# Low parts of the later weights by an accumulating DMA onto the negated high part, in place of a VectorE subtraction

## The chip, the cores and the metric

The kernel runs on one core of one Trainium2 chip. The metric is the device time of one execution in microseconds. A profile of one execution stands beside it: busy times of the engines (PE is TensorE's matmuls, DVE is VectorE, ACT is ScalarE, POOL is GpSimd, SP is SyncE, which only issues DMAs), waits, and the chain of work that ended last.

## The reference

One decoder block over 1024 tokens of width 1024, with a stick-breaking attention branch and a pooling branch. Cut to what matters here:

```python
h = rms_norm(x, norm_gain) * (1.0 + scale) + shift
proj = h @ w_in                                  # (1024, 1024) @ (1024, 8192)
q, k, v, z_a, u, z_b, m_a, m_b = split(proj)
attn = stick_breaking_attention(heads(q), heads(k), heads(v))
p_a = (attn * silu(z_a)) @ w_branch_a
p_b = (multiscale_causal_pool(u) * silu(z_b)) @ w_branch_b
out = x + gate * ((sigmoid(m_a) * p_a + sigmoid(m_b) * p_b) @ w_out)
return rms_norm(out, final_gain)
```

## The kernel before

**Products in two parts.** Every matrix is kept as a high part, the value rounded to the float32r format, and a low part, value minus high. A product is three matmuls into one sum: high by high, high by low, low by high (`mm3`). A column block of `w_in` is 128 columns wide, so as a tile it is 128 partitions by 1024 numbers, 512 KB. Its product with all tokens is two halves (`sh`) of 512 tokens, each 24 matmuls into one PSUM bank.

**Stages, in the order of PE.** First h and the folded u weights, then the second half of the u products (`u7_1` down to `u0_1`), then v (16 blocks `v0_0` to `v7_1`, 24 matmuls each), then z_b (`wzb0_0`, `wzb0_1` to `wzb7_1`), then w_branch_b (`pb0_0` to `pb7_1`), then attention together with the remaining 40 column blocks of `w_in`, then the branches and the output. The results of u, v, z_b, pb and the attention projections go through a tag `pj` with two PSUM banks: a product can begin only when the one two before it has been evicted. For v, ACT casts the bank to the high part (L610, `vo`) and DVE subtracts (L611). For z_b, ACT takes the sigmoid of the bank (L635, `zs`), and DVE multiplies the bank with it (L636), which is the last read of the bank.

**Low parts made early.** Of the 40 column blocks for the attention stage, the low parts of the last 32 (`l8` to `l39`) are made while u, v, z_b and pb run. They are written to a DRAM tensor `wl_d` and read back much later (L171, from 491.5 us on). This is the job of `make_lo`. For each tile, SP loads the block into `raw` (L152); ACT casts it to `hi` (L155); DVE subtracts and leaves the low part in `raw` (L156); SP stores `raw` to `wl_d` (L157). Eight tiles are asked for beside u and ten beside v (list `LO_V`, twice), from a pool with three buffers `lraw` and one buffer `lhi`; four beside z_b (`LO_ZB`), with two `lraw` and one `lhi`; ten beside pb (`LO_PB`), where raw and hi share a ring of five buffers with the tag `d`. With one `lhi`, the next cast waits until everything that reads or writes the previous `hi` is over: before, that is the subtraction L156.

**Order.** Outside the parts that the code pins, a scheduler puts each engine's instructions into an order when the program is built, by its own estimate of when each could run. That order is then fixed: an instruction that waits holds up all that stand behind it on its engine, and a DMA whose data isn't ready holds up its issuing queue. POOL's other work in this region is the low part of the w_branch_b tiles (`wb`, L118) and little else.

Of the kernel before, what the change touches and what calls it, by code (L numbers as in the profile page):

```python
# [9 lines left out]
F32 = mybir.dt.float32  # L10
F32R = mybir.dt.float32r
AF = mybir.ActivationFunctionType
ALU = mybir.AluOpType
# [44 lines left out]
def block_kernel(ctx, tc, a, out):  # L58
    nc = tc.nc
    v, act, gp = nc.vector, nc.scalar, nc.gpsimd  # L60
# [22 lines left out]
    wl_d = dram.tile([5 * KB, P, D], F32, name="wl_d")  # L83
# [58 lines left out]
    def make_lo(pl, n, tag=None, bufs=3, later=False):  # L142

        rest = []
        for _ in range(n):
            i = next(early_lo)
            if tag:
                raw, hi = (pl.tile([P, D], t_, tag=tag, bufs=5, name=f"l{i}_{n_}") for n_, t_ in (("raw", F32), ("hi", F32R)))
            else:
                raw = pl.tile([P, D], F32, tag="lraw", bufs=bufs, name=f"l{i}_raw")  # L150
                hi = pl.tile([P, D], F32R, tag="lhi", bufs=1, name=f"l{i}_hi")
            nc.sync.dma_start(raw, a["w_in"][tiles[i]])  # L152

            def low(i=i, raw=raw, hi=hi):
                act.copy(hi, raw)  # L155
                v.tensor_sub(raw.bitcast(F32R), raw, hi.bitcast(F32))  # L156
                nc.sync.dma_start(wl_d[i], raw)  # L157

            if later:
                rest.append(low)  # L160
            else:
                low()
        return rest
# [51 lines left out]
    with pool("init") as init:  # L215
# [168 lines left out]
        hi, lo_ = (0,), (1,)  # L384
# [719 lines left out]
```

## Time and profile before

| | us |
|---|---|
| device time, median of 3 runs | 1210.2 (1209.76 to 1210.31) |
| span of the profiled execution | 1210.3 |
| PE busy in it | 1199.2 |
| DVE busy | 756.5 |
| ACT busy | 531.6 |
| POOL busy | 187.2 |
| ACT's 32 casts L155, mean of one | 1.05 |
| DVE's 32 subtractions L156, mean of one | 1.22 |

The span is the profiled execution's own time; it lies inside the range of the timed runs, so nothing has to be added to it. PE busy is a sum over all stages, and the other engines' shares are averages over stages that need them differently: the tables by stretch of time show each stage by itself. The early low parts lie between 68.8 us (first load) and about 330 us (last store). In every view below, times are counted from the start of the span.

### The profile page before, as it was taken

The numbers are of one execution on the slowest core, as the hardware profiler recorded it, in microseconds if no ns is written. First come the engines' busy times: TensorE is split into PE (matmuls) and PEld (weight loads), VectorE is DVE, ScalarE is ACT, GpSimd is POOL, SyncE is SP. The second block draws the span as 40 slices with busy tenths as digits, with TensorE's granted clock in tenths as the row PEclk, the third lists the DMA queues.
The fourth block names the chain that finished last, engine by engine and source line by source line (L and its number), as shares of the span: only waits on it lengthen the run. The fifth ranks groups of instructions, "written<-read, shape, count | busy, mean of one in ns | idle before, by whom it ended". The sixth has DMA issues, their size and how long they took to land.

```text
span 1210.3 us, 16177 instructions
## 1 busy us (share of the span) xinstructions
PE 1199.2 (99%) x5746; PEld 1002.5 (83%) x5746; DVE 756.5 (63%) x1050; ACT 531.6 (44%) x1008; POOL 187.2 (15%) x360
## 2 busy tenths in 40 slices
PE   8999999999999999999999999999999999999997
PEld 7888878888888888888888888888888888888886
DVE  5764483677510286767868677686777853785643
ACT  5564331334301255655555555655555643232211
POOL 1000000001221333212222222222221210000001
PEclk9999999999999999999999999999999999999999
DMA  9649995626847632442635325353343344975622
GB/s 358 255 171 325 328 356 207 209 87 225 309 148 120 191 91 76 124 122 86 170 109 156 113 80 153 110 157 118 102 134 101 99 131 167 353 272 170 216 67 83
DMA packets 81955, 207.14 MB, mean 171 GB/s; under 512 B 10449, under 2 KB 23889, under 8 KB 79698
## 3 DMA queue, kind: packets, MB, share of 16 engines
q1 hardware_dynamic: 73666, 191.23, 49.2%
q10 hardware_dynamic: 8208, 14.88, 3.3%
q8 instruction: 45, 0.74, 0.2%
q14 instruction: 36, 0.29, 0.1%
HBM read 138.96 MB, written 50.34 MB: 156 GB/s over the span
## 4 chain that ended last, share of the span: by engine, by line
PE 88%; DMA 5%; issue 3%; DVE 2%; ACT 1%; POOL 0%; POOLq 0%; ACTq 0%; DVEq 0%; SPq 0%
PE p L103 34%; PE pb L103 7%; PE wzb L103 7%; PE pa L103 7%; PE o L103 6%; PE z L103 6%; PE av L103 5%; PE wt L103 5%; PE v L103 4%; PE ua L103 3%; DMA wl_d<-l_raw 2%; DMA l_raw<-in_w_in 2%; PE u L103 2%; PE wm L103 1%; DVE l_raw L156 1%
## 5 line engine op out<-in xcount | busy, mean ns | idle before, releaser
L103 PE MATMUL p<-hT,w 128*128 128x512 f32 x1920 | 480.0, 391 | 0.5 <-ACT m_sg L201 0.5
L103 PEld LDWEIGHTS p<-hT,w 128*128 128x128 f32 x1920 | 355.2, 188 | 74.7 <-ACT m_sg L201 1.0
L826 DVE TENSOR_TENSOR_SCAN om<-om 128x512 f32<-128x512 f32 (+7 forms) x128 | 175.8, 1373 | 124.9 <-ACT om L819 69.4
L819 ACT ACTIVATE om<-z 128x512 f32<-128x512 f32 (+2 forms) x192 | 94.5, 492 | 155.9 <-PE z L103 133.5
L824 POOL TENSOR_SCALAR_AFFINE_SELECT om<-om 128x128 f32<-128x128 f32 x128 | 56.3, 440 | 346.5 <-ACT om L819 287.0
L846 DVE TENSOR_TENSOR wt<-wt,wt 128x512 fp32r<-128x512 f32 (+1 forms) x160 | 99.3, 621 | 16.1 <-ACT wt L845 15.5
L845 ACT CAST wt<-wt 128x512 fp32r<-128x512 f32 (+1 forms) x160 | 88.2, 551 | 48.1 <-PE wt L103 47.9
L103 PE MATMUL av<-wt,vv 128*128 128x512 f32 x320 | 106.4, 414 | 0.0
L103 DVE TENSOR_TENSOR be<-be,om 128x511 f32<-128x511 f32 (+7 forms) x128 | 95.1, 749 | 1.1 <-POOL be L824 0.7
L820 ACT ACTIVATE be<-z 128x512 f32<-128x512 f32 (+2 forms) x192 | 94.1, 490 | 0.0
L103 PE MATMUL pa<-ga,wa 128*128 128x512 f32 x384 | 89.6, 389 | 0.1
L103 PE MATMUL o<-wo,mhl 128*128 128x512 f32 (+1 forms) x408 | 89.6, 377 | 0.0
L103 PE MATMUL wt<-ident,be 128*128 128x128 f32 x576 | 89.4, 273 | 0.0
L103 PE MATMUL v<-wv,hT 128*128 128x512 f32 x384 | 87.8, 390 | 0.5 <-DVE vo L611 0.5
L103 PE MATMUL wzb<-hT,wzb 128*128 128x512 f32 x384 | 87.2, 389 | 0.0
L103 PE MATMUL pb<-gb,wb 128*128 128x512 f32 x384 | 87.2, 389 | 0.0
L103 PEld LDWEIGHTS v<-wv,hT 128*128 128x128 f32 x384 | 71.9, 188 | 16.2 <-DVE vo L611 1.4
L103 PEld LDWEIGHTS o<-wo,mhl 128*128 128x128 f32 x408 | 73.5, 188 | 14.1
L103 PEld LDWEIGHTS pa<-ga,wa 128*128 128x128 f32 x384 | 72.0, 188 | 15.4 <-DVE wa L118 0.5
L103 PEld LDWEIGHTS wzb<-hT,wzb 128*128 128x128 f32 x384 | 72.1, 188 | 14.9
L103 PEld LDWEIGHTS pb<-gb,wb 128*128 128x128 f32 x384 | 72.1, 188 | 14.9
L103 PEld LDWEIGHTS wt<-ident,be 128*128 128x128 f32 x576 | 70.2, 141 | 11.6
(130 smaller groups left out, 1364.5 us busy)
## 6 DMA issues: line engine op xcount, KB each, us to landing
w_raw<-in_w_in SPq DMA_DIRECT2D x40, 512.0 KB, 4.7
l_raw<-in_w_in SPq DMA_DIRECT2D x32, 512.0 KB, 5.2
wl_d<-l_raw SPq DMA_DIRECT2D x32, 512.0 KB, 5.7
w<-wl_d SPq DMA_DIRECT2D x32, 512.0 KB, 3.8
v_d<-vo SPq DMA_DIRECT2D x16, 512.0 KB, 5.2
vv<-v_d SPq DMA_DIRECT2D x8, 1024.0 KB, 5.3
wa_raw<-in_w_branch_a SPq DMA_DIRECT2D x16, 512.0 KB, 4.7
wa<-in_w_mod SPq DMA_DIRECT2D x7, 1024.0 KB, 6.4
```

The costliest lines, as they stand in the source:

```text
L103: ins = op(*args, **kw)
L156: v.tensor_sub(raw.bitcast(F32R), raw, hi.bitcast(F32))
L819: act.activation(om[:, b0:b0 + n], zp[:, :n], AF.Sigmoid, scale=-0.125)
L820: act.activation(be[:, b0:b0 + n], zp[:, :n], AF.Sigmoid, scale=0.125)
L824: gp.affine_select(out=tl[:, :P], in_=tl[:, :P], pattern=[[1, P]], compare_op=ALU.is_gt, fill=fill, base=0, channel_multiplier=-1)
L826: v.tensor_tensor_scan(om[:, :W], om[:, :W], om[:, :W], 1.0, ALU.mult, ALU.min)
L845: act.copy(wt[:, 0, :off], pt[:, :off])
L846: v.tensor_sub(wt[:, 1, :off], pt[:, :off], wt[:, 0, :off].bitcast(F32))
```

## The change

In `make_lo`, ACT writes the negative of the rounded tile to `hi` instead of the rounded tile. POOL then issues a DMA that adds `raw` onto `hi`, in SBUF, which leaves raw minus high in `hi`. SP stores `hi` to `wl_d`, where it stored `raw` before. DVE has no part in it any more. The pools, the numbers of buffers and the places where `make_lo` is called are the same.

```diff
             def low(i=i, raw=raw, hi=hi):
-                act.copy(hi, raw)
-                v.tensor_sub(raw.bitcast(F32R), raw, hi.bitcast(F32))
-                nc.sync.dma_start(wl_d[i], raw)
+                act.mul(hi, raw, -1.0)
+                gp.dma_start(hi.bitcast(F32), raw, accum_op=ALU.add)
+                nc.sync.dma_start(wl_d[i], hi.bitcast(F32))
```

So `hi` is now in use from the multiplication through the accumulating DMA until the store has been read out of it, and with one `lhi` the next tile's multiplication waits for the end of that store. `raw` is free when the accumulating DMA has ended.

PE's order is the same as before. On ACT, the 18 tiles `l8` to `l25` begin at the same place (behind the cast of `wv0_1`) but are spread further. This is ACT at the end of the v stage and the beginning of z_b, before:

```order
L610 CAST vo5_1_1643<-v5_1_1618 128x8x64
L610 CAST vo6_1_1675<-v6_1_1650 128x8x64
L610 CAST vo7_1_1710<-v7_1_1685 128x8x64
L155 CAST l26_hi_1857<-l26_raw_1856 128x1024
L155 CAST l27_hi_1997<-l27_raw_1996 128x1024
L635 ACTIVATE zs0_0_1722<-wzb0_0_1729 128x512
L638 CAST gb_1721<-zs0_0_1722 128x512
L635 ACTIVATE zs0_1_1723<-wzb0_1_1759 128x512
```

And now:

```order
L610 CAST vo6_1_1675<-v6_1_1650 128x8x64
L155 ACTIVATE l20_hi_1394<-l20_raw_1393 128x1024
L610 CAST vo7_1_1710<-v7_1_1685 128x8x64
L155 ACTIVATE l21_hi_1464<-l21_raw_1463 128x1024
L155 ACTIVATE l22_hi_1537<-l22_raw_1536 128x1024
L123 CAST wzb2_1866<-wzb2_raw_1864 128x1024
L155 ACTIVATE l23_hi_1572<-l23_raw_1571 128x1024
L155 ACTIVATE l24_hi_1648<-l24_raw_1647 128x1024
L155 ACTIVATE l25_hi_1680<-l25_raw_1679 128x1024
L635 ACTIVATE zs0_0_1722<-wzb0_0_1729 128x512
L635 ACTIVATE zs0_1_1723<-wzb0_1_1759 128x512
L155 ACTIVATE l26_hi_1857<-l26_raw_1856 128x1024
```

Before, tile 25 was cast ahead of the last seven evictions of v, and only tiles 26 and 27 stood here; now tiles 21 to 25, all on the one `lhi`, stand between the last eviction of v and the first of z_b.

A little further on, ACT in the z_b stage before (columns as above; `gjunk` is a sigmoid of a row needed for the output gate):

```order
L155 CAST l29_hi_2337<-l29_raw_2336 128x1024
L635 ACTIVATE zs1_1_1790<-wzb1_1_1826 128x512
L123 CAST wzb3_1933<-wzb3_raw_1931 128x1024
L638 CAST gb_1721<-zs1_0_1789 128x512
L635 ACTIVATE zs2_0_1862<-wzb2_0_1869 128x512
```

And now:

```order
L635 ACTIVATE zs1_1_1790<-wzb1_1_1826 128x512
L123 CAST wzb3_1933<-wzb3_raw_1931 128x1024
L638 CAST gb_1721<-zs1_1_1790 128x512
L155 ACTIVATE l28_hi_2165<-l28_raw_2164 128x1024
L635 ACTIVATE zs2_0_1862<-wzb2_0_1869 128x512
L638 CAST gb_1721<-zs2_0_1862 128x512
L635 ACTIVATE zs2_1_1863<-wzb2_1_1899 128x512
L123 CAST wzb4_2020<-wzb4_raw_2018 128x1024
L155 ACTIVATE l29_hi_2337<-l29_raw_2336 128x1024
L638 CAST gb_1721<-zs2_1_1863 128x512
L647 ACTIVATE gjunk_2343<-sg_2342 128x1024
L635 ACTIVATE zs3_0_1929<-wzb3_0_1936 128x512
```

Tiles 27, 28 and 29 now stand between evictions of blocks 1 and 3, one at a time; tile 29 is three half blocks later, ahead of the eviction `zs3_0`. Beyond, `l30` stands behind `zs4_1`, `l31` behind `zs5_1`, and `l39` behind the eviction of `pb2_0`.

On POOL, the difference at the only place that changes (the `st` rows belong to the first stage, the `wb` rows to pb):

```order
 L258 TENSOR_TENSOR st_638<-st_638,mhalf 128x1
+L156 DMA l_hi<-l_raw 128x1024 x25
 L118 TENSOR_TENSOR wb_2354<-wb_raw,wb_2354 128x1024
+L156 DMA l_hi<-l_raw 128x1024 x2
 L118 TENSOR_TENSOR wb_2424<-wb_raw,wb_2424 128x1024
```

25 accumulating DMAs stand ahead of the first `wb` low part, and the last seven between the `wb` low parts that follow.

## The prediction, made before the changed kernel was run

> **What bounds the kernel now.** The page comes first, then what PE waited for, then a table by stretch of time.
>
> ```profile
> span 1210.3 us, 16177 instructions
> PE 1199.2 (99%) x5746; PEld 1002.5 (83%) x5746; DVE 756.5 (63%) x1050; ACT 531.6 (44%) x1008; POOL 187.2 (15%) x360
> ```
> ```profile
> PE idle L103 <- POOL x L243: 1.6, 1, 1.6
> PE ua L103 <- ACT hT L103: 1.1, 1, 1.1
> PE ua L103 <- DVE wg L103: 1.0, 1, 1.0
> PE p L103 <- ACT m_sg L201: 0.5, 1, 0.5
> PE v L103 <- DVE vo L611: 0.5, 2, 0.3
> ```
> ```profile
> 95.00:145.00 50.00, 50.00 (x221) 41.09 (x220) 20.30 (x20) 19.61 (x24) 0.00 (x0) 1.00 0.93 331
> 145.00:195.00 50.00, 49.47 (x218) 40.31 (x217) 38.12 (x53) 16.07 (x21) 0.00 (x0) 1.00 0.99 346
> 195.00:240.00 45.00, 45.00 (x200) 37.30 (x199) 19.77 (x25) 12.28 (x18) 0.00 (x0) 1.00 0.52 176
> 240.00:290.00 50.00, 50.00 (x223) 41.40 (x222) 36.02 (x48) 18.75 (x28) 0.00 (x0) 1.00 0.37 119
> ```
>
> PE is busy all but 11.1 us of the span. Where the early low parts are made (the table's columns are length, then PE, weight loads, DVE, ACT and POOL busy, then the granted clock, the DMA engines' share and GB/s), PE loses 0.5 us in all, waiting for DVE in the v stage. So all that the change can win by freeing DVE is **0.5 us**, though it takes 32 subtractions off it. What decides is what the new chain does to PE through ACT.
>
> **The chain of one low part.** The instructions of `l_raw` (durations as least, median, greatest; then first and last start), and a piece of the chain that ended last, with the PE stages behind it:
>
> ```profile
> L155 ACT CAST l_hi<-l_raw x32: 1040/1051/1058, 90.7 to 323.9; 128x1024 fp32r<-128x1024 f32 x32
> L156 DVE TENSOR_TENSOR l_raw<-l_raw,l_hi x32: 1207/1224/1279, 92.1 to 325.0; 128x1024 fp32r<-128x1024 f32 x32
> DMA to landing us min/median/max: 2.6/5.3/9.2
> ```
> ```profile
> 95.41 1.06 ACT l_hi L155
> 96.47 0.02 issue
> 96.49 1.24 DVE l_raw L156
> 97.73 0.01 issue
> 97.74 5.66 DMA wl_d<-l_raw
> ...
> 172.87 43.81 PE v L103 x192
> 216.69 87.04 PE wzb L103 x384
> 303.73 87.04 PE pb L103 x384
> ```
>
> Before, `hi` was busy for cast and subtraction, 1.05 + 1.22 = 2.3 us a tile, and the store ran from `raw`, of which there are three. Now `hi` is held for the multiplication, the accumulating DMA (A, issue to landing) and the store (S, issue to landing), and the pool of tiles 8 to 25 has one `hi`. So the multiplications of two neighbours can't be closer than T = 1.05 + A + S + 0.15, where 0.15 is three hand-overs of some 0.05 us (the "issue" and queue pieces in that chain are 0.01 to 0.04 each). The negation is taken at the cast's 1.05 us. DVE loses 32 × 1.22 = 39 us of work, all beside a PE that did not wait for it.
>
> **A and S.** The trace has no accumulating DMA. The nearest rows are these (form, count, KB each, median us to landing), the last one from a view of 195 to 290 us alone:
>
> ```profile
> l_raw<-in_w_in SPq DMA_DIRECT2D x32, 512.0 KB, 5.2
> wl_d<-l_raw SPq DMA_DIRECT2D x32, 512.0 KB, 5.7
> vv<-v_d SPq DMA_DIRECT2D x8, 1024.0 KB, 5.3
> wa<-in_w_mod SPq DMA_DIRECT2D x7, 1024.0 KB, 6.4
> kh<-kh SPq DMA_DIRECT2D x48, 128.0 KB, 3.7
> ```
> ```profile
> wl_d<-l_raw SPq DMA_DIRECT2D x6, 512.0 KB, 3.0
> ```
>
> S was 5.7 us in the median and 3.0 where the DMA engines were about half idle (share 0.52 and 0.37 above). A slower chain stretches the same traffic over more time, so I take the middle, **4.35**, with 3.0 and 5.7 as ends. For A, 512 KB from `raw` and 512 KB of old `hi` are read and 512 KB are written. Not less than the 3.7 us that an SBUF to SBUF move of 128 KB took; not more than twice the 6.4 us of a 1024 KB transfer, 12.8, as if reading and writing back didn't overlap. I take the 1024 KB transfer of a full stage, **6.4**, since a megabyte is read. T is then 1.05 + 6.4 + 4.35 + 0.15 = **11.95 us**, with ends 7.9 and 19.7.
>
> The page "DMA: Bandwidth & Descriptors" of the Trainium skill (section "Anatomy of one DMA — SWDGE (gpsimd) path") fits a DMA issued by GpSimd as 2.0 us plus bytes over 436 GB/s; by it a plain 512 KB copy would be 3.2 us, an estimate, T 8.75, and the time 1241 by the sums below. No run here shows such a DMA yet.
>
> **The v stage and the step into z_b.** These rows of ACT's and DVE's instructions anchor the sum (start, us, what; the last row is durations of the bank's last read):
>
> ```profile
> 90.67 1.05 ACT L155 CAST l_hi<-l_raw 128x1024 fp32r<-128x1024 f32 x1
> 216.73 0.59 ACT L610 CAST vo<-v 128x512 fp32r<-128x512 f32 x1 [4.85 <-PE v L103]
> 222.17 0.60 ACT L635 ACTIVATE zs<-wzb 128x512 f32<-128x512 f32 x1 [0.66 <-PE wzb L103]
> 255.56 1.06 ACT L647 ACTIVATE gjunk<-sg 128x1024 f32<-128x1024 f32 x1
> ```
> ```profile
> L636 DVE TENSOR_TENSOR zs<-wzb,zs x16: 672/688/693, 222.8 to 307.8; 128x512 f32<-128x512 f32 x16
> ```
>
> The first tile is cast at 90.67 in a place that the new order keeps. Tile 25 is 17 periods later, and only behind it does ACT evict `zs0_0`: 1.05 for tile 25, 0.60 for the sigmoid, 0.69 for DVE's read, 2.34 together, and the bank is free for `wzb1_0`. A half block of z_b takes 87.04 / 16 = 5.44 us, so PE wants that bank at 216.69 + 2 × 5.44 = 227.57. PE comes late by
>
> (a) 90.67 + 17 T + 2.34 − 227.57 = 17 T − 134.6, at T = 11.95 **68.6 us**.
>
> There is a second bound. Tiles 21 to 25 stand behind `vo7_1`, which can't be evicted before PE has made v; undisturbed that eviction ended at 216.73 + 0.59 = 217.32. Four periods follow:
>
> (b) 217.32 + 4 T + 2.34 − 227.57 = 4 T − 7.9, at 11.95 39.9 us.
>
> The larger holds; they cross at T = 9.74. In (a) part of the delay builds up inside v: a multiplication that waits keeps the `vo` casts behind it, and with two banks PE stands. SP's queue should keep up: a store waits there for its accumulation, and behind it stand the stores of v, the load of the tile three periods on, and in places a weight load of z_b (that of `wzb4` behind the store of tile 21), needed two blocks later.
>
> **z_b itself.** From the release of that bank PE has six half blocks, 32.64 us, until `wzb4_0` needs the bank of `zs3_0`. ACT has tiles 26 to 29 before `zs3_0`: four periods, then 1.05, `gjunk` 1.06, 0.60 and 0.69. Counted from tile 25 that is 4 T + 3.40 against 2.34 + 32.64 = 34.98. Tile 26 has another `hi`, but its load is issued behind tile 25's store, so its distance is 1.05 + A + 5.2 + 0.15, 0.85 more than T. Together 4 T − 31.6 + 0.85 = **17.1 us**.
>
> **pb.** Tiles 31 to 39 go round a ring of five buffers, two each, so 2.5 are under way: 5.2 (load) + 1.05 + A + S = 17.0 us a round, 6.8 a tile, 54.4 for eight. PE has `wzb6` to `pb1`, 4 × 10.88, and `pb2_0`, and one half block in the other bank: 54.4. This costs nothing at my values, 24.8 us at the upper ends. POOL's first `wb` low part, until now preceded by 227.5 idle us, comes behind accumulation 32, two blocks ahead of its use; what is covered by these two blocks would cost the excess alone.
>
> ```profile
> 294.34 3.27 POOL L118 TENSOR_TENSOR wb<-wb_raw,wb 128x1024 fp32r<-128x1024 f32 x1 [227.47 <-DVE wb L127]
> ```
>
> From then on PE runs as before, later by the sum, and the read back of `wl_d` moves with it. **Sum:** 68.6 + 17.1 + 0 − 0.5 = 85.2 us on the span of 1210.3, which is the timed median within 0.1: 1295.5, given as **1295 us**.
>
> One more rule is weighed. The DVE row of L156 is 1.22 us for 1024 numbers, and GpSimd did nothing from 66.9 to 294.3 us (the idle time in the row above), so no row shows the two against each other. The page "SBUF — State Buffer" of the Trainium skill (section "SBUF: two separate sides") says that a DMA issued from GpSimd can starve, since GpSimd can't write descriptors while DVE runs certain fast copies. If every accumulation waited for one DVE instruction of 1.22 us, 21 periods would add 25.6 us and the time would be 1321; it lies within the forecast's own band, and on the side of a longer A.
>
> **The rivals.**
>
> *Short accumulation.* If T is 7.9 to 9.74, the chain from 90.67 is not what binds, but tiles 21 to 25 still stand before `zs0_0`. (b) gives 23.7 to 31.1, z_b 0.9 to 8.2; less 0.5 that is 1234 to 1249. For it: the move of 128 KB in 3.7 and the store of 3.0. Against it: six times the bytes (1536 KB read and written for 256), and a stage with the DMA engines at 0.93 to 0.99.
>
> *Long accumulation.* If the sums in flight run at a fraction of the copies' rate, T goes from 15 to 19.7. At 15 (a) gives 120.4, z_b 29.3, the ring 9.8 with A 9.0 and S 4.8: 1369. At the ends, 200.3 + 48.1 + 24.8 − 0.5 makes 1483. For it: landings of up to 9.2 us among these tiles, and a kind of DMA the trace doesn't have. Against it: traffic spreads out as PE slows.
>
> *Not slower.* The place is ACT between `vo7_1` and `zs0_0`. If the five multiplications there could run without waiting for DMAs, z_b's banks would come free in time. It decides at 4 T = 7.9, T = 1.98; then the delay is gone and the 0.5 us of DVE stays: 1209.8. Against it: none of these 512 KB transfers landed under 2.6 us, and each `hi` is read by one and written by another. That POOL doesn't take over the work at all is in this case too; the 25 and 7 issues in POOL's order speak against it.
>
> **How the numbers follow.** Forecast (T 9.74 to 15, 1249 to 1369) 0.60; short 0.17; long 0.20; not slower 0.03, of which 0.01 over 0.2% faster and 0.02 within. About 0.2% is what a measurement of this kernel can tell from no change. All other cases are slower, 0.97. For 8 in 10 the range takes the forecast, the short case down to 1234, and the nearer part of the long one to 1410, leaving out not slower and what lies beyond.
>
> **What would show it.** In the changed kernel's chain that ended last, ACT `l_hi`, DMA `l_hi` and DMA `wl_d` should take turns from about 91 us on, and multiplications of tiles 8 to 25 be T apart, 11 to 13 us. The v stage should end late already, and PE stand longest before `wzb1_0`, for ACT or DVE's `zs`, with smaller gaps to `wzb4_0`; pb and all after should take as long as before. DVE's 32 rows of L156 should be gone. It is wrong if A is not between 4 and 10 us, if v runs undisturbed (then only (b) is left), or if PE waits for weights, which would mean SP's queue, held by a store, is the bound and not ACT.

## The result, and the profile after

| | before | changed |
|---|---|---|
| device time, median (us) | 1210.3 | 1276.1 (4 runs, 1272.8 to 1280.7) |
| ratio, 95% interval | | 1.054 [1.052, 1.057], slower |
| span of the profiled execution (us) | 1210.3 | 1273.5 (device time of this execution 1275.2) |
| PE busy in it (us) | 1199.2 | 1207.2 |

One of the four executions of the kernel before took 4418.2 us, and the ratio leaves it out (the other three: 1209.76 to 1210.31). The forecast was 1295 us in a range of 1234 to 1410, slower with a chance of 0.97. These are the first lines of the page of the changed kernel, the clock by slices, and its two largest groups of DMA queues:

```profile
span 1273.5 us, 16222 instructions
PE 1207.2 (95%) x5746; PEld 1003.8 (79%) x5746; DVE 720.3 (57%) x1018; ACT 531.0 (42%) x1008; POOL 215.5 (17%) x392
...
PEclk9999999769999999999999999999999999999999
...
q1 hardware_dynamic: 73666, 191.23, 46.9%
q0 software_dynamic: 4608, 16.78, 6.9%
```

DVE is 36 us less busy, which nobody waited for, and PE has the same 5746 matmuls. The line q0 is new (packets, MB, share of 16 DMA engines): the 32 accumulating DMAs. What PE waits for between 60 and 500 us (total, times, longest), where it was 0.5 us before, and PE's work in time order (start, us, what, idle before it):

```profile
PE wzb L103 <- DVE zs L636: 45.1, 4, 39.1
PE v L103 <- DVE vo L611: 7.2, 5, 2.4
PE pb L103 <- ACT sm L661: 1.7, 2, 1.3
```
```profile
224.99 11.04 PE L103 MATMUL wzb<-hT,wzb 128*128 128x512 f32 x48
275.17 13.37 PE L103 MATMUL wzb<-hT,wzb 128*128 128x512 f32 x48 [39.13 <-DVE zs L636]
291.18 11.18 PE L103 MATMUL wzb<-hT,wzb 128*128 128x512 f32 x48 [2.63 <-DVE zs L636]
304.97 11.17 PE L103 MATMUL wzb<-hT,wzb 128*128 128x512 f32 x48 [2.62 <-DVE zs L636]
316.88 43.81 PE L103 MATMUL wzb<-hT,wzb 128*128 128x512 f32 x192 [0.74 <-DVE zs L636]
360.95 5.05 PE L103 MATMUL pb<-gb,wb 128*128 128x512 f32 x21 [0.26 <-DVE zs L636]
...
454.65 25.32 PE L103 MATMUL p<-hT,w 128*128 128x512 f32 x111
```

`wzb1_0` starts at 275.17; undisturbed it would be 227.57 by the prediction's count, so PE is **47.6 us** late there. `wzb4_0` starts at 316.88 against 227.57 + 6 × 5.44 = 260.21, 56.7 late: z_b adds **9.1**. Stage pb, from 360.95 to 454.65, takes 93.7 us, where it took 87.0: **6.7**. With 0.7 more at the end of z_b that is 64.1; some 0.9 comes back later, and the span is 63.2 us longer.

A piece of the chain that ended last shows what PE waited for, then the group of ACT's multiplications (busy, mean ns; idle before, and what ended most of it), the landings of tiles 8 to 25 (KB each, median us), and ACT at the last of these tiles, ahead of the first evictions of z_b:

```profile
129.62 5.00 DMA l_hi<-l_raw
...
134.63 3.46 DMA wl_d<-l_hi
...
138.18 1.07 ACT l_hi L155
...
139.53 5.57 DMA l_hi<-l_raw
```
```profile
L155 ACT ACTIVATE l_hi<-l_raw 128x1024 fp32r<-128x1024 f32 x32 | 33.9, 1059 | 175.8 <-DMA wl_d<-l_hi 120.1
```
```profile
l_hi<-l_raw POOLq DMA_DIRECT2D x18, 512.0 KB, 5.0
l_raw<-in_w_in SPq DMA_DIRECT2D x17, 512.0 KB, 4.8
wl_d<-l_hi SPq DMA_DIRECT2D x17, 512.0 KB, 3.0
```
```profile
272.85 1.06 ACT L155 ACTIVATE l_hi<-l_raw 128x1024 fp32r<-128x1024 f32 x1 [7.60 <-DMA wl_d<-l_hi]
273.81 1.07 ACT L635 ACTIVATE zs<-wzb 128x512 f32<-128x512 f32 x2
```

Multiplication, accumulation and store take turns, as in the prediction. Tile 8 is multiplied at 90.85 and tile 25 at 272.85, so T is (272.85 − 90.85) / 17 = **10.7 us**, and the prediction's formula (a) gives 17 × 10.71 − 134.6 = 47.5 us for the 47.6 measured. From here it looks as if one sentence were enough: one high buffer, held for 10.7 us a tile, ahead of the evictions on ACT. The experiments ask whether that sentence holds.

### The profile page after: what moved, and what is told of

It reads as the page before. It is cut to its first block, busy times and chain, and to the rows that moved or that the text cites. A ratio compares the mean times of both kernels' runs of the same rounds, so it can differ in the third digit from the quotient of the medians.

```text
span 1273.5 us, 16222 instructions
## 1 busy us (share of the span) xinstructions
PE 1207.2 (95%) x5746; PEld 1003.8 (79%) x5746; DVE 720.3 (57%) x1018; ACT 531.0 (42%) x1008; POOL 215.5 (17%) x392
## 3 DMA queue, kind: packets, MB, share of 16 engines
q1 hardware_dynamic: 73666, 191.23, 46.9%
## 4 chain that ended last, share of the span: by engine, by line
PE 72%; DMA 19%; issue 3%; DVE 2%; ACT 2%; SPq 0%; POOL 0%; POOLq 0%; ACTq 0%; DVEq 0%
PE p L103 35%; DMA l_hi<-l_raw 12%; PE pa L103 7%; PE o L103 6%; PE av L103 5%; PE z L103 5%; PE wt L103 5%; DMA wl_d<-l_hi 5%; PE pb L103 4%; DMA l_raw<-in_w_in 3%; PE ua L103 2%; PE wm L103 1%; ACT l_hi L155 1%; PE wzb L103 1%; DVE hT L549 0%
## 5 line engine op out<-in xcount | busy, mean ns | idle before, releaser
L103 PE MATMUL wzb<-hT,wzb 128*128 128x512 f32 x384 | 90.6, 397 | 45.1 <-DVE zs L636 45.1
L155 ACT ACTIVATE l_hi<-l_raw 128x1024 fp32r<-128x1024 f32 x32 | 33.9, 1059 | 175.8 <-DMA wl_d<-l_hi 120.1
L103 PE MATMUL pb<-gb,wb 128*128 128x512 f32 x384 | 90.2, 395 | 3.9 <-ACT sm L661 1.7
```

The lines of the kernel that those rows point to most:

```text
L103: ins = op(*args, **kw)
L155: act.mul(hi, raw, -1.0)
```

## Experiments

Every ratio is against runs of the kernel before on the same chip (medians 1210.3 to 1211.4 us). **T** is from the starts of tile 8 and tile 25, divided by 17.

| run | us | ratio, 95% interval | T, us |
|---|---|---|---|
| changed | 1276.1 | 1.054 [1.052, 1.057] | 10.7 |
| e1_onto_raw | 1256.4 | 1.037 [1.034, 1.040] | 9.0 |
| e2_two_hi | 1238.5 | 1.022 [1.020, 1.024] | 8.3 |
| e3_traffic | 1238.2 | 1.022 [1.021, 1.024] | 8.4 |
| e4_store_hi | 1211.9 | 1.001 [1.000, 1.002] | 7.0 |
| e5_last10 | 1217.6 | 1.005 [1.004, 1.007] | 5.2 |
| e6_first18 | 1267.2 | 1.047 [1.045, 1.049] | 10.7 |
| e9_idle_copy | 1218.5 | 1.007 [1.005, 1.008] | 7.4 |
| e10_pool_mul | 1279.2 | 1.056 [1.053, 1.058] | 11.1 |
| e11_own_pool | 1250.3 | 1.032 [1.029, 1.034] | 10.8 |
| e12_own_pool_pool_mul | 1264.4 | 1.044 [1.043, 1.046] | 11.5 |
| e13_before_own_pool | 1220.1 | 1.008 [1.006, 1.009] | 6.8 |
| e14_all_on_pool | 1220.9 | 1.009 [1.007, 1.010] | 12.5 |

In the kernel before, T is 5.4 us (90.67 to 182.50).

### The long hold of the one high buffer

Four runs take the accumulation, the buffers and the source of the store apart.

**e1_onto_raw**: the DMA adds the negated high part onto `raw`, of which there are three, so that `hi` is free after the accumulation, and the store leaves from `raw` as before.

```diff
-                gp.dma_start(hi.bitcast(F32), raw, accum_op=ALU.add)
-                nc.sync.dma_start(wl_d[i], hi.bitcast(F32))
+                gp.dma_start(raw, hi.bitcast(F32), accum_op=ALU.add)
+                nc.sync.dma_start(wl_d[i], raw)
```

> The sum goes the other way round: the DMA adds the negated high part onto raw, of which there are three, and raw is stored. The same DMAs, the same bytes; hi is free when the accumulation has landed, so the period falls from 1.06 + A + S to about 1.06 + 0.35 + 5.0 = 6.5 us. Theory (one hi, held until its store has landed, holds ACT and with it the evictions): 17 periods end at 90.7 + 110 = 201, before ACT gets there, v is undisturbed; tiles 24 and 25 behind the last eviction of v cost nothing, tiles 27 to 29 some us in z_b, the ring of five in pb a few: 1210 to 1222. Rival (the added DMA traffic slows the stage, whoever waits): as much traffic as in the changed kernel, so 40 us or more stay: 1250 to 1276.

**e2_two_hi**: the changed kernel with two `lraw` and two `lhi` in the pool of v, in the same memory.

```diff
-                raw = pl.tile([P, D], F32, tag="lraw", bufs=bufs, name=f"l{i}_raw")
-                hi = pl.tile([P, D], F32R, tag="lhi", bufs=1, name=f"l{i}_hi")
+                raw = pl.tile([P, D], F32, tag="lraw", bufs=2, name=f"l{i}_raw")
+                hi = pl.tile([P, D], F32R, tag="lhi", bufs=bufs - 1, name=f"l{i}_hi")
```

> The changed kernel with one buffer moved in the pool of tiles 8 to 25: two hi and two raw in place of one and three. Everything else is as changed, in z_b one hi and in pb the ring. Theory: two chains side by side, one tile about every 5 to 6 us; v undisturbed, the 39 us wait ahead of wzb1_0 gone; z_b at one hi but spread by the order so that 10 us a tile fit between its evictions; pb costs its 6 to 7 us as in the changed kernel: 1212 to 1224. Rival (traffic): 1250 to 1276.

**e3_traffic**: the kernel before, with an accumulating DMA of the same size behind DVE's subtraction. It adds a slice of h onto `raw`, so the low parts, and with them the output, are off by that slice.

```diff
                 v.tensor_sub(raw.bitcast(F32R), raw, hi.bitcast(F32))
+                gp.dma_start(raw, h_hi[:, i % KB].bitcast(F32), accum_op=ALU.add)
                 nc.sync.dma_start(wl_d[i], raw)
```

> The kernel before with an accumulating DMA of 512 KB added to every tile: behind DVE's subtraction, POOL adds a slice of h onto raw, which is then stored; so the low parts are wrong by that slice. hi is busy for cast and subtraction alone (2.3 us), raw (three buffers) is held longer. Theory: ACT waits for no accumulation, so PE is undisturbed in v and z_b; the ring in pb may cost what it costs in the changed kernel: 1210 to 1220. Rival (traffic): 40 us or more over the kernel before, 1250 and up.

**e4_store_hi**: no accumulating DMA; DVE subtracts into `hi`, and the store leaves from `hi`.

```diff
-                v.tensor_sub(raw.bitcast(F32R), raw, hi.bitcast(F32))
-                nc.sync.dma_start(wl_d[i], raw)
+                v.tensor_sub(hi, raw, hi.bitcast(F32))
+                nc.sync.dma_start(wl_d[i], hi.bitcast(F32))
```

> No accumulating DMA: the kernel before, but DVE's subtraction writes into hi and the store is from hi, so hi is held for cast, subtraction and store, 1.05 + 1.22 + 3 to 5 us of store, a period of 5.4 to 7.5 us. Theory: too short to bind at 17 periods (90.7 + 17 x 6.5 = 201), so within some 10 us of the kernel before: 1210 to 1220. If the store alone in the chain is what costs (a rival on which part of the chain matters), it is 1230 or more.

e4 came out as expected: a high buffer that is held through its store makes T 7.0 us and costs some 2 us at most. The other three did not: they lost 27 to 45 us, far from the 1210 to 1224 that were expected. e1 even fell into the band of the rival, which puts the loss down to the added traffic, and e2 and e3 lie between the two bands, so these runs alone leave that rival open. ACT's waits ahead of its casts say why, first e1's, then e2's, then e3's, and last the landings in e3:

```profile
ACT l_hi L155 <- DMA l_raw<-l_hi: 81.9, 16, 9.5
```
```profile
ACT l_hi L155 <- DMA l_raw<-in_w_in: 87.0, 24, 9.1
```
```profile
ACT l_hi L155 <- DMA l_raw<-in_w_in: 102.3, 22, 10.9
```
```profile
l_raw<-hT POOLq DMA_DIRECT2D x32, 512.0 KB, 7.7
wl_d<-l_raw SPq DMA_DIRECT2D x32, 512.0 KB, 6.6
l_raw<-in_w_in SPq DMA_DIRECT2D x31, 512.0 KB, 6.1
```

In e1 the one `hi` is still held until the accumulation has read it. In e2 and e3, where `hi` is no longer the bound, the ring of raw buffers is: in e3 a raw buffer is in use for load, cast, subtraction, accumulation and store, 6.1 + 2.3 + 7.7 + 6.6 = 22.7 us, and with three of them a tile can't come oftener than every 7.6 us (T was 8.4). So an accumulation lengthens whichever ring it stands in. Formula (a) with the measured T gives 18.7, 6.7 and 8.6 us for `wzb1_0` in e1, e2 and e3; it started at 247.88, 237.29 and 238.49, which is 20.3, 9.7 and 10.9 us late. The formula holds within 3 us; what fell was the expectation that a second high buffer undoes the loss. The rest of these runs' loss lies in z_b and pb.

### Where in the program

**e5_last10** takes the accumulating DMA for the ten tiles beside pb alone (`if tag:`), **e6_first18** for tiles 8 to 25 alone (`if i < 26:`); the other tiles are made as before.

> Only the last ten tiles (the ring of five of the pb stage) take the accumulating DMA; the 22 before them are as before. Theory A (the loss comes from casts on ScalarE that are held and stand ahead of evictions; the ring of five holds nothing): at most the 6.5 us that the pb stage lost in the changed kernel, so 1210 to 1218 us. Theory B (the accumulating DMA costs in proportion to the transfers, wherever they stand): ten of the 32 tiles, 10 x 2.0 us = 20 us, so about 1230 us.

> Only tiles 8 to 25 (u and v stages) take the accumulating DMA; z_b's four and the last ten are as before. Theory A: the 47.6 us before wzb1_0 stays, z_b's 9.1 and pb's 6.5 go: 1250 to 1266 us. Theory B (in proportion): 18 x 2.0 = 37 us, 1247 us. Together with the run on the last ten it shows whether the stages add up to the 65 us of the whole change.

They lost 6.2 and 55.9 us, 62.1 together, against 64.7 to 65.9 for the whole. In proportion to the tiles it would have been 20 and 37, so the place decides. e6 lies 1 us above theory A's band. PE of e6 at the end of v and in z_b:

```profile
275.53 13.84 PE L103 MATMUL wzb<-hT,wzb 128*128 128x512 f32 x48 [38.88 <-DVE zs L641]
292.31 68.35 PE L103 MATMUL wzb<-hT,wzb 128*128 128x512 f32 x288 [2.95 <-DVE zs L641]
360.50 87.20 PE L103 MATMUL pb<-gb,wb 128*128 128x512 f32 x384
```

pb is undisturbed, so the changed kernel's 6.7 us there come from the last ten tiles. But z_b still loses 8.8 us (360.50 against 303.73 is 56.8, of which 48.0 stood before `wzb1_0`), though its own four tiles are made by DVE again. The total is nearly that of the changed kernel, but it is made of other parts: there PE waits 2.63, 2.62 and 0.74 us ahead of `wzb2_0`, `wzb3_0` and `wzb4_0`, in e6 2.95 us once, and the other 5.9 us are matmuls that take longer after the stop (13.84 us for two half blocks of 5.44, and 68.19 us from 292.31 to 360.50 for twelve).

### Traffic, or waiting in an order?

**e9_idle_copy**: the kernel before, and a copy of each stored low part to another DRAM tensor that nothing reads.

```diff
                 nc.sync.dma_start(wl_d[i], raw)
+                gp.dma_start(junk_d[i], wl_d[i])
```

> The kernel before, and after each low part's store one more copy of 512 KB from DRAM to DRAM that nothing waits for (1.64 us of all DMA engines each by the rate of plain copies, 30 us for the 18 tiles of the u and v stages). Theory A (half of the loss is the room on the DMA engines): loads and stores grow, ScalarE's casts come late and hold evictions, 1218 to 1235 us. Theory B (traffic that nobody waits for costs nothing, the loss is the chain of waits alone): 1208 to 1214 us.

**e10_pool_mul**: the changed kernel with the multiplication on GpSimd, off ACT's queue.

```diff
-                act.mul(hi, raw, -1.0)
+                gp.tensor_scalar(hi, raw, -1.0, 0.0, op0=ALU.mult, op1=ALU.add)
...
-            whl = load_w(a["w_branch_b"][j], f"wb{j}", v, gp)
+            whl = load_w(a["w_branch_b"][j], f"wb{j}", v, v)
```

> The changed kernel, but GpSimd makes the negated high part, not ScalarE, and VectorE takes the low parts of w_branch_b that GpSimd made; the transfers and the buffers stay as in the changed kernel. Theory A (the loss reaches PE only through ScalarE's queue, where held casts stand ahead of evictions): the periods of a tile stay at 8 to 12 us, but PE's 39 us before wzb1_0 go: 1208 to 1225 us. Theory B (the full DMA engines delay the weights of v, z_b and pb themselves): PE waits for weights, 1235 to 1280 us.

e9 lost 7.1 us, at the low end of theory A's band and above theory B's: traffic that nothing waits for isn't free, but it costs a small part of the 66 us. The 32 copies took 3.9% of the span (q0, 1.5 us of all 16 engines each), little more than half of the accumulations' 6.9%, so the run doesn't settle the question by itself. In e9 the scheduler also put some casts later on ACT, so it is not traffic alone. e10 came out as neither theory had it: its time lies in theory B's band, but PE waits for DVE's `zs` and not for weights. ACT holds no multiplication any more, and PE's wait ahead of `wzb1_0` is down to 3.13 us from 39.13; but a wait as long now stands one block later, ahead of `wzb2_0`:

```profile
246.09 12.76 PE L103 MATMUL wzb<-hT,wzb 128*128 128x512 f32 x48 [3.13 <-DVE zs L636]
297.53 67.16 PE L103 MATMUL wzb<-hT,wzb 128*128 128x512 f32 x288 [38.68 <-DVE zs L636]
```

Its chain, from the multiplication of tile 25 on, shows why:

```profile
279.07 1.04 POOL l_hi L155
...
280.46 4.60 DMA l_hi<-l_raw
...
285.07 3.04 DMA wl_d<-l_hi
...
288.96 0.63 ACT gb L638
...
289.61 0.69 DVE gb L639
```

The **first write of `gb`** waits for the store of tile 25. No data goes from the one to the other: `gb` (64 KB a partition, pool of pb) lies on memory of the pool of v, and with it on `lraw` and `lhi`. (In e11 and e12 below, where it lies elsewhere, no write of `gb` waits for a DMA.) Behind that write, on ACT and on DVE, stands the eviction of `wzb1_0`, which frees the bank for `wzb2_0`. The first hold ends with the multiplication of tile 25, the second with its store, 9.0 us later, so taking ACT's away uncovered it.

### Taking the holds away one after the other

**e11_own_pool**: the changed kernel with `lraw` (two) and `lhi` (one) of tiles 8 to 29 in a pool of their own, open through v and z_b, so that `gb` lies elsewhere. **e12_own_pool_pool_mul**: e11 and e10 together. **e13_before_own_pool**: the kernel before with that pool, as a control.

```diff
+    los = ExitStack()
+    lo = los.enter_context(pool("lo"))
     with pool("vp") as vp:
...
-            make_lo(vp, 1)
+            make_lo(lo, 1, bufs=2)
...
-                now, todo = todo, make_lo(vp, LO_V[sb], later=True)
+                now, todo = todo, make_lo(lo, LO_V[sb], bufs=2, later=True)
...
-            make_lo(pb, LO_ZB[j], bufs=2)
+            make_lo(lo, LO_ZB[j], bufs=2)
```

> The changed kernel with the same high-part buffer, but the raw and high buffers of tiles 8 to 29 lie in a pool of their own (two raw, one high) that stays open through v and z_b, so that gb, which z_b writes first, no longer lies on them and need not wait for the last low part of v. The multiplication stays on ScalarE. Theory C (two holds of equal standing: ScalarE's order, and the memory of v's pool that gb takes over): the second is gone, the first stays in part, 1225 to 1265 us. Theory A (ScalarE's order alone): 1265 to 1280 us, no gain. Theory D (the memory alone): 1209 to 1220 us.

> As the run with the pool of its own, and GpSimd makes the negated high part (VectorE the low parts of w_branch_b), so that no cast stands on ScalarE either. All 32 accumulating DMAs, one high buffer and the periods of 8 to 12 us stay. Theory C (two holds): both gone, PE's 39 us before wzb1_0 go, 1209 to 1222 us. Theory B (the full DMA engines delay weights that PE waits for): 1235 to 1280 us.

> Control: the kernel before with the same pool of its own (two raw buffers in place of three). All theories: 1209 to 1214 us; above that, the third raw buffer is worth something to it.

e11 fell into the band of two holds: T is 10.8 as in the changed kernel, yet the loss is 40 us and not 66. The scheduler also spread the multiplications among the evictions here, so the memory's share can't be told from the order's. The control lost 9.6 us: it has two raw buffers in v for three, and PE waits 6.8 us there. e12 was a miss again, 1264 for an expected 1209 to 1222; the time lies in theory B's band, but PE waits for DVE's `zs`, not for weights. PE's, SP's and DVE's waits in it, and SP's issues and DVE's work around PE's first stop in z_b:

```profile
PE wzb L103 <- DVE zs L638: 29.2, 3, 14.4
```
```profile
SPq L157 <- DMA l_hi<-l_raw: 171.0, 23, 10.3
```
```profile
DVE gjunk L659 <- DMA wg<-in_w_gate: 27.7, 2, 20.0
DVE win L569 <- DMA u<-u_d: 16.8, 1, 16.8
```
```profile
260.82 0.32 SPq L157 DMA_DIRECT2D wl_d<-l_hi  x1
...
262.54 0.41 SPq L560 DMA_DIRECT2D u<-u_d  x1
```
```profile
268.81 1.24 DVE L569 TENSOR_TENSOR win<-u 128x1039 f32<-128x1039 f32 x1 [16.76 <-DMA u<-u_d]
269.97 0.68 DVE L638 TENSOR_TENSOR zs<-wzb,zs 128x512 f32<-128x512 f32 x1
```

That is a **third queue**. SP's stores of low parts wait in order for their accumulations, 171 us in all. Behind one of them stands the load of `u`, issued at 262.54; it lands some 6 us later, DVE's pooling begins at 268.81, and the eviction that stands behind it, at 269.97, frees PE's bank, so that PE goes on at 270.71 after 13.7 us. PE's other long stop, 14.4 us, comes the same way: DVE's row of the gate waits 20.0 us for its load `wg`, issued at 332.40 behind a store that SP held for its accumulation until 331.48, and evictions of z_b stand behind that row.

**e14_all_on_pool**: e12, and GpSimd's queue also issues the raw load and the store of tiles 8 to 29, so that only GpSimd ever waits for them. The last ten tiles are made as before.

```diff
-            nc.sync.dma_start(raw, a["w_in"][tiles[i]])
+            (nc.sync if tag else gp).dma_start(raw, a["w_in"][tiles[i]])
...
-                nc.sync.dma_start(wl_d[i], hi.bitcast(F32))
+                    gp.dma_start(wl_d[i], hi.bitcast(F32))
```

> As the run with the pool of its own and the multiplication on GpSimd, and GpSimd's queue also issues the raw load and the store of tiles 8 to 29, so that SP's queue holds no step of them either; the last ten tiles are made as in the kernel before. The 22 accumulating DMAs, one high buffer and a period of 10 to 13 us stay; GpSimd is through at about 90 + 22 x 12.5 = 365 us, ahead of its next work for p. Theory C (the period costs only what stands behind a tile's steps in an in-order queue; SP's queue was the third, held 171 us on accumulations in the run before this): PE's waits before wzb blocks go, 1210 to 1224 us. Theory B (the full DMA engines delay the transfers that PE's work needs): PE still stands over 20 us there, 1235 to 1280 us.

It took 1220.9 us, in the expected band, and within the intervals no more than its control, e13. PE's waits, and GpSimd's:

```profile
PE wzb L103 <- DVE zs L643: 3.1, 1, 3.1
PE v L103 <- DVE vo L618: 2.2, 3, 0.9
```
```profile
POOL wl_d L162 <- DMA l_hi<-l_raw: 133.0, 22, 9.7
POOL l_hi L160 <- DMA wl_d<-l_hi: 79.4, 21, 6.4
```

T is 12.5 us, longer than in the changed kernel, the 22 accumulations land in 6.2 us at the median, and GpSimd waits 212 us for the chain. PE waits 5.3 us. So neither the accumulating DMA, nor its traffic, nor the length of the chain costs 60 us with these 22 tiles: the **waiting in queues that PE's evictions also use** does. Two things differ from e12: the queue, and the last ten tiles. By e5 the tiles are worth about 6 of the 43 us between the two, and the waits that went, 29.2 to 3.1 us before z_b's blocks, lie ahead of them.

## Why the prediction was right, step by step

- **The sign and the mechanism: right.** The chain of three, the place ahead of `wzb1_0`, the late end of v (224.99 for 216.53), the wait for DVE's `zs` and DVE's missing rows came as written. With the measured T, formula (a) is right within 0.1 us; since T is taken from the starts of the same tiles 8 and 25, that tests the step from tile 25 to PE, not T.
- **T: 11.95 forecast, 10.7 measured; this term carries most of the 19 us of error.** For tiles 8 to 25 the accumulation landed in 5.0 us at the median where 6.4 was taken, the store in 3.0 for 4.35. By the medians T would be 1.05 + 5.0 + 3.0 + some 0.5 of hand-overs = 9.5; five accumulations of 7.4 to 10.0 us before 193 us, and waits for raw loads, made the mean 10.7. At 17 periods, 1.24 us are 21 us. The other two terms, z_b 8.0 us too long and pb 6.7 too short, nearly cancel, which is luck.
- **z_b: 17.1 forecast, 9.1 measured; a size, and not the only cause.** With the measured starts the prediction's own sum gives 8.0: tile 29 was multiplied at 312.43, 39.58 us behind tile 25, and 39.58 + 3.40 − 34.98 = 8.0. PE did wait there for DVE's `zs` (0.74 us ahead of `wzb4_0`). But e6 has none of z_b's own accumulations and loses 8.8: 2.95 us of waiting and 5.9 us of matmuls that take longer after the stop. The prediction had no term for those.
- **pb: 0 forecast, 6.7 measured; a size.** The ring of five was right, its round too short: in e5 load, accumulation and store landed in 6.0, 6.7 and 5.7 us around pb, 19.5 us a round with the multiplication for the 17.0 taken, so 7.8 us a tile for eight tiles, 62.3 less 54.4 = 7.9 us. Measured were 5.6 (e5) to 6.7.
- **"SP's queue should keep up": true only behind a longer wait.** In the changed kernel ACT's multiplications hold first, but SP waits for accumulations there too (total, times and longest in the row below), and with ACT and `gb` out of the way PE waits 29.2 us ahead of z_b's blocks (e12).

```profile
SPq L157 <- DMA l_hi<-l_raw: 144.0, 25, 9.6
```

- **The rival "not slower" was put too simply.** It said that the delay is gone if the multiplications ahead of `zs0_0` run without waiting. In e10 they aren't on ACT at all; the delay ahead of `wzb1_0` goes, and one of 38.68 us comes ahead of `wzb2_0`: the memory under `gb` was in no step of the prediction.
- **Short and long accumulation:** T lies between their bounds; formula (b), 4 × 10.7 − 7.9 = 34.9, stayed under (a).
- **Rules that were weighed.** The page "DMA: Bandwidth & Descriptors" of the Trainium skill (section "Anatomy of one DMA — SWDGE (gpsimd) path") would have a plain copy of this size land in 3.2 us, an estimate by its fit. In e14, where GpSimd issues the plain stores, they landed in 3.0 us at best and 4.5 at the median; the accumulations of the changed kernel landed in 4.5 at best. For the accumulation the measurement decides. The page "SBUF — State Buffer" of the Trainium skill (section "SBUF: two separate sides") has GpSimd's descriptors starve under certain fast copies of DVE. No row here shows that: with DVE busy 28.6 of 38 us, an accumulation of e12 landed as fast as any:

```profile
268.00:306.00 38.00, 34.16 (x141) 27.84 (x142) 28.60 (x35) 11.39 (x17) 7.23 (x7) 0.91 0.78 229
```
```profile
285.84 4.58 DMA l_hi<-l_raw
```

**What stays open:** how much of the loss in the changed kernel is each queue's. They stand in parallel, so each hides the others, and the shares found by taking them away depend on the sequence. Likewise how the slower matmuls and z_b's own tiles share the 9.1 us of the changed kernel. No version here is faster than the kernel before; DVE's subtraction was hidden, so there was 0.5 us to win.

## What to carry to other kernels

Here a step that was moved from an engine to a DMA turned a computation of 1.2 us into a wait of 4.5 to 10 in every in-order queue that held a later step of the same chain. Before such a move, list these queues: the engine that waits for the buffer, the queue that issues the store and the next load, and whatever later takes over the buffers' memory; in e14 a slow chain cost no more than its control, with one otherwise nearly idle engine issuing all of it and nothing else on its memory (T of 12.5 us, PE waits of 5.3). When an experiment that takes away the one wait you see wins nothing, look for a second that ends close behind the first (9.0 us in e10) before giving up the mechanism.

## What the runs showed of the hardware

- An accumulating DMA of 512 KB within SBUF took 6.9% × 1273.5 / 32 = 2.75 us of all 16 DMA engines. A plain transfer of that size took 46.9% × 1273.5 / (191.23 / 0.524) = 1.64 us by the mean of queue q1. The accumulation landed in 4.5 us at best, between 225 and 275 us, where the DMA engines were busy 0.67 of the time, and in 10.0 us at most, the first one, at 92.23 us.
- GpSimd needed 0.86 to 1.05 us to issue one (0.56 for a plain store in e14).
- After the stop of 39 us PE's next 48 matmuls took 13.37 us for 11.04. The table by stretches (length, PE, weight loads, DVE, ACT, POOL busy, granted clock, DMA share, GB/s) has the clock there:

```profile
225.00:275.00 50.00, 11.03 (x49) 8.82 (x47) 2.50 (x3) 8.72 (x10) 5.11 (x6) 0.64 0.67 183
275.00:317.00 42.00, 35.84 (x145) 28.52 (x146) 27.45 (x39) 12.82 (x18) 3.62 (x5) 0.94 0.73 208
```

In e6 the 336 matmuls of z_b behind a stop of 38.88 us took 5.9 us more than undisturbed, with this row among them:

```profile
293.00:300.00 7.00, 7.00 (x22) 5.52 (x21) 6.21 (x9) 4.05 (x5) 0.00 (x0) 0.62 0.60 218
```

So these waits of PE cost a little more than their length: 2.3 us on top of 39 in the changed kernel, 5.9 in e6.
